# Gates and ups of the first feed-forward by seven block products from the third pair of tiles on

## The chip, the cores and the metric

One Trainium2 chip; the kernel runs on one of its cores. The metric is the time of one execution on the device, in microseconds (us), as the median of several runs.

## The reference

One layer of an encoder on 784 tokens (16 meta tokens, 512 of a prompt, 256 of a sample), model width 1024, feed-forward width 2816, all in float32. What matters here, shortened:

```python
def rmsnorm(x, w):
    return x * lax.rsqrt(jnp.mean(x * x, axis=-1, keepdims=True) + EPS) * w

def swiglu(u, wg, wu, wd):
    return (jax.nn.silu(u @ wg) * (u @ wu)) @ wd

h += 0.5 * swiglu(rmsnorm(h, w1), wg1, wu1, wd1)     # first feed-forward, 784 tokens
u = rmsnorm(h, w_mix)                                # mixer: attention and a state space model
h += concat(diff_attention(u ...), ssd_mixer(u ...)) @ w_out
h += 0.5 * swiglu(rmsnorm(h, w2), wg2, wu2, wd2)     # second feed-forward, 768 tokens
y = rmsnorm(h, w_final)
```

## The kernel before

Features lie on the partitions, tokens along the free axis. The model width is 8 tiles of 128 (k), the feed-forward width 22 tiles in 11 pairs. The tokens are cut into two halves of 392 columns in the first feed-forward (784 tokens) and of 384 in the second (768).

**Products.** A float32 product is three matmuls of rounded numbers: each operand is split into a high part (ACT casts, line 182) and a low part (DVE subtracts, line 183), and `mm3` (lines 316 to 318) issues high x high, low x high and high x low. One unit of a gate or up is one feature tile by one token half: 8 k tiles, 24 matmuls into one PSUM bank (`ps_mm` or `ps_x`).

**Weights.** `Weights` loads them by SP's DMA queue in pieces of 512 KB (`wr`, two buffers) and splits them into `wh` and `wl` (four buffers). `pump`, called by `done()` after every unit, splits one job ahead when buffers are free. `done()` also moves every generator on the `agenda` one step: the norms, parameters and transfers that run beside the products. The order on an engine follows from this order of the program, which a scheduler lays out by priority.

**First feed-forward**, `ffn`. The activation goes into the products as h times the norm's weight (tiles `u1`); the token's factor (`rms1`, tile `w3_136` in the order) is multiplied in behind the gate: DVE multiplies (line 453), ACT does silu (454), DVE multiplies again (455). Ups: DVE multiplies the gate by the up (460) and the result is split into high and low parts. `BOUNDS` puts the pairs into groups [0], [1, 2], [3, 4], [5, 6], [7, 8], [9, 10]. The down product of a group comes after the first pair of the next group, and DVE adds it to h (line 480). Pair 0 runs on three parts of the tokens (272, 256, 256 columns), since the tokens are only just being loaded and normed.

**Second feed-forward**, `ffn_fast`. The first pair is plain; the others go through `quad`, which takes a block of two feature tiles, two halves of k and two token halves and computes it from seven products of 12 matmuls instead of eight (`p1`, `p6`, `p5`, `p2`, `p7`, `p3`, and `p4`, which is issued behind the first product of the next block). It needs sums of weight blocks (jobs `a` to `d` of `split_fast`, sums on DVE in lines 255 to 260) and of activation blocks (`t2`, `n1`, `m3`, `m4`, built once in `FastNorm.chain`), and combines the products on DVE (lines 652 to 688). A group's down product follows directly on its blocks (line 699).

**Memory.** One pool per stretch of the program: tags `w3`, `w4`, `f3` and so on in the pool `mix`, which lasts from the start to the second feed-forward's end.

**Parameters.** `parameters()` loads the small inputs, makes the lambda products (lines 925, 926), the relative position table `fv` (lines 930 to 932, 31 small copies) and its eight spread copies `fr_d` (520 KB each), all on the agenda of the first feed-forward.

Of the kernel before, what the change touches and what calls it, by code (L numbers as in the profile page):

```python
# [14 lines left out]
P = 128  # L15
# [32 lines left out]
def body(tc, x_prompt, x_sample, meta_tokens, ffn1_norm_w, ffn1_w_gate, ffn1_w_up, ffn1_w_down,  # L48
# [34 lines left out]
    next_stretch("mix")  # L83
# [4 lines left out]
    def f3(n, dt=F32):  # L88
        return stretch_pool[0].tile([P, XW + 1], dt, tag="f3", name="f3", bufs=18)[:, :n]

# [30 lines left out]
    BOUNDS = [0, 1, 3, 5, 7, 9, NPAIR]  # L121
# [19 lines left out]
    def plan_ffn_fast(f, wg, wu, wd):  # L141
        for g in range(len(BOUNDS) - 1):
            for pr in range(BOUNDS[g], BOUNDS[g + 1]):
                for key, src in (("g", wg), ("u", wu)):
                    (plan_fast if pr else plan_w8)((f, key, pr), src, pr * 256)
            plan_down(f, wd, g)

    def plan_ffn(f, wg, wu, wd):
        for g in range(len(BOUNDS) - 1):
            for i, pr in enumerate(range(BOUNDS[g], BOUNDS[g + 1])):  # L150
                plan_w8((f, "g", pr), wg, pr * 256)
                plan_w8((f, "u", pr), wu, pr * 256)
                if i == 0 and g > 0:
                    plan_down(f, wd, g - 1)
        plan_down(f, wd, len(BOUNDS) - 2)

    def plan_down(f, wd, g):
        k0, k1 = 2 * BOUNDS[g], 2 * BOUNDS[g + 1]
        for cp in range(KD // 2):
            plan_1((f, "d", g, cp), wd, k0, k1 - k0, cp * 256, 256)  # L160
# [18 lines left out]
    plan_ffn_fast(2, ffn2_w_gate[0], ffn2_w_up[0], ffn2_w_down[0])  # L179
# [17 lines left out]
    class Weights:  # L197
# [43 lines left out]
        def split_fast(self, key, kind, raw, hi, lo):  # L241
# [99 lines left out]
    def diags(r, tiles):  # L341

        dg = w3()
# [86 lines left out]
    def ffn(f, h, halves, u, after, first=None, last=None, rms=None):  # L430

        g_t = {}

        def gate_up(pr):
            sg = {}
            w = {}
            parts = (first or halves) if pr == 0 else halves
            end = len(parts) - 1

            def unit(which, m, i):  # L440
                o, n = parts[i]
                if which not in w:
                    w[which] = W.get8((f, "gu"[which], pr))
                ps = ps_any()
                dense(ps[:, :n], w[which], m, u(i if pr == 0 else None), o, n)
                if which == 0:
                    if i == 0:
                        sg[m] = w3()
                    t = sg[m][:, o:o + n]
                    if rms is None:  # L450
                        S.activation(t, ps[:, :n], AF.Silu)
                    else:
                        V.tensor_tensor(t, ps[:, :n], rms[:, o:o + n], ALU.mult)  # L453
                        S.activation(t, t, AF.Silu)  # L454
                        V.tensor_tensor(t, t, rms[:, o:o + n], ALU.mult)
                else:
                    if i == 0:
                        g_t[2 * pr + m] = [w4(T1, F32R), w4(T1, F32R)]
# [1217 lines left out]
```

## Time and profile before

| | |
|---|---|
| median of 3 runs | 1880.02 us (1877.45 to 1881.81) |
| the profiled execution | 1877.39 us |
| its span in the trace | 1875.7 us |
| mean granted clock of TensorE | 0.991 of full speed |
| busy share of the span: PE, DVE, ACT, POOL | 97%, 63%, 40%, 5% |
| first feed-forward | from about 20 to 575 us |
| second feed-forward | from about 1330 us to the end |

The profile is of one execution. PE is TensorE's matmuls, DVE VectorE, ACT ScalarE, POOL GpSimd, SP the engine that issues the DMAs here. A group of instructions has a line of the kernel, an operation, its tiles (out<-in), a count, busy time and mean duration, and the idle time of the engine ahead of its members with the engine that ended most of it. A duration is that of one instruction; neighbours overlap, so the distance of their starts is shorter.

### The profile page before, as it was taken

The numbers are of one execution on the slowest core, as the hardware profiler recorded it, in microseconds if no ns is written. First come the engines' busy times: TensorE is split into PE (matmuls) and PEld (weight loads), VectorE is DVE, ScalarE is ACT, GpSimd is POOL, SyncE is SP. The second block draws the span as 40 slices with busy tenths as digits, with TensorE's granted clock in tenths as the row PEclk, the third lists the DMA queues.
The fourth block names the chain that finished last, engine by engine and source line by source line (L and its number), as shares of the span: only waits on it lengthen the run. The fifth ranks groups of instructions, "written<-read, shape, count | busy, mean of one in ns | idle before, by whom it ended". The sixth has DMA issues, their size and how long they took to land.

```text
span 1875.7 us, 27520 instructions
## 1 busy us (share of the span) xinstructions
PE 1825.0 (97%) x10934; PEld 1756.2 (94%) x10934; DVE 1175.6 (63%) x2305; ACT 748.2 (40%) x1486; POOL 93.8 (5%) x118
## 2 busy tenths in 40 slices
PE   7999999999999999989899999999999999999998
PEld 7999999999998998878798988999989999999997
DVE  6454333443436489676787878674897575757573
ACT  6222121212123452667556767343334241414144
POOL 0000000000003000123100000001100000000002
PEclk9999999999999999999899999999999999999999
DMA  4152212221222223797541334321112121222121
GB/s 139 58 172 68 66 47 68 68 61 52 71 64 93 68 65 93 184 232 202 161 140 50 89 98 151 134 88 43 35 57 90 46 90 53 83 57 80 56 79 68
DMA packets 161268, 169.77 MB, mean 91 GB/s; under 512 B 9921, under 2 KB 146234, under 8 KB 161138
## 3 DMA queue, kind: packets, MB, share of 16 engines
q1 hardware_dynamic: 161122, 168.00, 29.9%
q8 instruction: 86, 1.41, 0.3%
q14 instruction: 44, 0.36, 0.1%
q10 hardware_dynamic: 16, 0.00, 0.0%
HBM read 148.54 MB, written 22.87 MB: 91 GB/s over the span
## 4 chain that ended last, share of the span: by engine, by line
PE 83%; DVE 10%; ACT 3%; issue 2%; DMA 2%; POOL 0%; SPq 0%; ACTq 0%; POOLq 0%; DVEq 0%
PE ps_mm L316 13%; PE ps_mm L317 13%; PE ps_mm L318 13%; PE ps_x L316 10%; PE ps_x L318 10%; PE ps_x L317 9%; PE ps_s L316 2%; PE ps_s L317 2%; PE ps_s L318 2%; DVE w L1026 2%; PE ps_s L1462 2%; DMA w<-ar_d 1%; PE ps_s L1580 1%; ACT w L1209 1%; DVE wl L183 1%
## 5 line engine op out<-in xcount | busy, mean ns | idle before, releaser
L316 PE MATMUL ps_mm<-w,wh 128*128 128x384 f32 (+4 forms) x1520 | 518.7, 341 | 4.0 <-DVE w L1341 1.9
L317 PE MATMUL ps_mm<-w,wl 128*128 128x384 f32 (+4 forms) x1520 | 515.5, 339 | 4.3 <-DVE wl L183 4.3
L318 PE MATMUL ps_mm<-w,wh 128*128 128x384 f32 (+4 forms) x1520 | 516.5, 340 | 2.8 <-DVE w L183 2.2
L182 ACT CAST wh<-wr 128x1024 fp32r<-128x1024 f32 (+1 forms) x194 | 190.1, 981 | 312.0 <-PE ps_x L318 251.2
L316 PEld LDWEIGHTS ps_mm<-w,wh 128*128 128x128 f32 x1520 | 287.2, 189 | 10.7 <-issue 2.7
L316 PE MATMUL ps_x<-w,wh 128*128 128x392 f32 (+4 forms) x864 | 293.7, 340 | 0.9 <-ACT w L1107 0.9
L318 PEld LDWEIGHTS ps_mm<-w,wh 128*128 128x128 f32 x1520 | 287.1, 189 | 7.4 <-DVE w L183 3.3
L317 PEld LDWEIGHTS ps_mm<-w,wl 128*128 128x128 f32 x1520 | 287.3, 189 | 7.0 <-DVE wl L183 4.6
L317 PE MATMUL ps_x<-w,wl 128*128 128x392 f32 (+4 forms) x864 | 292.8, 339 | 0.0
L318 PE MATMUL ps_x<-w,wh 128*128 128x392 f32 (+4 forms) x864 | 292.3, 338 | 0.0
L183 DVE TENSOR_TENSOR wl<-wr,wh 128x1024 fp32r<-128x1024 f32 (+1 forms) x194 | 222.1, 1146 | 87.6 <-ACT wh L182 86.8
L316 PEld LDWEIGHTS ps_x<-w,wh 128*128 128x128 f32 x864 | 163.7, 189 | 2.1 <-ACT w L1107 1.2
L317 PEld LDWEIGHTS ps_x<-w,wl 128*128 128x128 f32 x864 | 163.8, 190 | 0.7
L318 PEld LDWEIGHTS ps_x<-w,wh 128*128 128x128 f32 x864 | 163.5, 189 | 0.7
L182 ACT CAST w<-w 128x392 fp32r<-128x392 f32 (+4 forms) x130 | 73.8, 570 | 202.4 <-DVE w L460 118.3
L183 DVE TENSOR_TENSOR w<-w,w 128x392 fp32r<-128x392 f32 (+4 forms) x130 | 83.4, 645 | 29.4 <-ACT w L182 28.5
L365 POOL TENSOR_TENSOR w<-w,w 128x392 f32<-128x392 f32 (+3 forms) x36 | 40.7, 1130 | 981.7 <-ACT w L364 981.7
L182 ACT CAST wh<-sums 128x1024 fp32r<-128x1024 f32 x40 | 42.0, 1051 | 108.7 <-PE ps_x L318 60.5
L1486 ACT ACTIVATE w<-w,nmx 128x528 f32<-128x528 f32 (+1 forms) x96 | 63.6, 664 | 40.0 <-DVE nmx L1482 31.0
L454 ACT ACTIVATE w<-w 128x392 f32<-128x392 f32 (+2 forms) x46 | 23.8, 516 | 112.8 <-DVE w L453 112.8
L183 DVE TENSOR_TENSOR wl<-sums,wh 128x1024 fp32r<-128x1024 f32 x40 | 49.0, 1225 | 29.6 <-ACT wh L182 29.6
L1209 ACT ACTIVATE w<-w,w 128x128 f32<-128x128 f32 x192 | 58.2, 389 | 15.4 <-POOL w L1205 15.4
(335 smaller groups left out, 2872.6 us busy)
## 6 DMA issues: line engine op xcount, KB each, us to landing
wr<-in_ffn_w_gate_dram SPq DMA_DIRECT2D x44, 512.0 KB
wr<-in_ffn_w_up_dram SPq DMA_DIRECT2D x42, 512.0 KB
wr<-in_w_in_dram SPq DMA_DIRECT2D x42, 512.0 KB
wr<-in_ffn_w_down_dram SPq DMA_DIRECT2D x40, 512.0 KB
w<-ar_d SPq DMA_DIRECT2D x24, 512.0 KB
wr<-in_w_out_dram SPq DMA_DIRECT2D x16, 512.0 KB
w<-ar_d SPq DMA_DIRECT2D x24, 256.0 KB
w<-q_d SPq DMA_DIRECT2D x32, 192.0 KB
```

The source lines that it names most:

```text
L182: a = S.copy(hi, src)
L183: return a, V.tensor_tensor(lo, src, hi.bitcast(F32), ALU.subtract)
L316: nc.tensor.matmul(ps, ah, bh, start=start, stop=False, skip_group_check=onto)
L317: nc.tensor.matmul(ps, al, bh, start=False, stop=False, skip_group_check=onto)
L318: last_mm[0] = nc.tensor.matmul(ps, ah, bl, start=False, stop=stop, skip_group_check=onto)
L365: G.tensor_tensor(sums[0], sums[0], sq, ALU.add)
L454: S.activation(t, t, AF.Silu)
L1026: V.scalar_tensor_tensor(acc, pad[:, j:j + XW], prmT[:, cw:cw + 1], acc, ALU.mult, ALU.add)
L1209: S.activation(ab[d][:, h, :], ab[d][:, h, :], AF.Exp, bias=ssm["asp"][:, c, col_s:col_s + 1])
L1462: nc.tensor.matmul(ps[:, b, :w], qh[c][part][:, P * i:P * i + P], kh[c][:, k0 + b * w:k0 + b * w + w], start=part == 0, stop=part == 1)
L1486: S.activation(e[:, :nk], e[:, :nk], AF.Exp, bias=nmx[:, c:c + 1], scale=-1.0, accum_out=(s0, s1)[c])
L1580: nc.tensor.transpose(ps[:n, 0, q * P:(q + 1) * P], A[q0 + q][:, c:c + n], ident)
```

## The change

One function `ffn` now serves both feed-forwards, as plain pairs first and then quads. `GROUPS` gives each its groups: the first feed-forward runs pairs 0 and 1 plain and pairs 2 to 10 as quads, the second as before. In the first, the gates keep their multiplication by the token's factor, now in `act`. A class `Blocks` builds the sums of the activations for the first feed-forward on the agenda, from the last part of pair 0 on, and writes `n1` over a part of `u1` behind pair 1. In `split_fast`, job `d` takes two sums instead of three by going on from job `b`'s. The memory of this stretch has a pool of its own (`f1s`, `f1g`, `f1t`), between one for the loading of the tokens and the mixer's. The lambda products use other tiles and come earlier; the table `fv` and the copies `fr_d` go from the first feed-forward to the mixer, behind `dt_unit`. The down product of a group follows directly on its blocks in both feed-forwards.

```diff
-    BOUNDS = [0, 1, 3, 5, 7, 9, NPAIR]
+    GROUPS = {1: [0, 2, 3, 5, 7, 9, NPAIR], 2: [0, 1, 3, 5, 7, 9, NPAIR]}
...
-                sums = stretch_pool[0].tile([P, 2 * 4 * P], F32, tag="sums", name="sums", bufs=1)
-                t = sums.rearrange("p (s k f) -> p s k f", s=2, k=4)
                 if kind == "b":
+                    sums = stretch_pool[0].tile([P, 2 * 4 * P], F32, tag="sums", name="sums", bufs=1)
+                    t = self.sums = sums.rearrange("p (s k f) -> p s k f", s=2, k=4)
                     V.tensor_tensor(t[:, 1], raw[0][:, :, y], raw[1][:, :, y], ALU.add)
                     V.tensor_tensor(t[:, 0], t[:, 1], raw[0][:, :, x], ALU.add)
                 else:
-                    V.tensor_tensor(t[:, 0], raw[0][:, :, x], raw[0][:, :, y], ALU.add)
-                    V.tensor_tensor(t[:, 1], raw[1][:, :, x], raw[1][:, :, y], ALU.add)
-                    V.tensor_tensor(t[:, 1], t[:, 0], t[:, 1], ALU.add)
+                    t, self.sums = self.sums, None
+                    V.tensor_tensor(t[:, 1], raw[0][:, :, x], raw[0][:, :, y], ALU.add)
+                    V.tensor_tensor(t[:, 0], t[:, 0], raw[1][:, :, x], ALU.add)
...
+        def act(t, src, o, n):
+            if rms is None:
+                S.activation(t, src, AF.Silu)
+            else:
+                V.tensor_tensor(t, src, rms[:, o:o + n], ALU.mult)
+                S.activation(t, t, AF.Silu)
+                V.tensor_tensor(t, t, rms[:, o:o + n], ALU.mult)
...
+        for pr in range(bounds[0], bounds[1]):
+            plain(pr)
+        norm.ready()
         down(0)
-        norm.B[1][:4] = [None] * 4
-        for g in range(1, len(BOUNDS) - 1):
+        for g in range(1, len(bounds) - 1):
             late = None
-            for pr in range(BOUNDS[g], BOUNDS[g + 1]):
+            for pr in range(bounds[g], bounds[g + 1]):
                 for which in range(2):
                     steps = quad(which, pr)
...
+    class Blocks:
...
+        def split(self, key, t, pair=None):
...
+            S.copy(hi, t)
+            V.tensor_tensor(lo, t, hi.bitcast(F32), ALU.subtract)
...
+        def first_sum(self, k):
+            a = f1(2 * self.n)
+            b12, n1 = a[:, :self.n], a[:, self.n:]
+            x, w = self.part(k, 1)
+            S.activation(b12, x, AF.Copy, scale=w)
+            x, w = self.part(k, 0)
+            V.scalar_tensor_tensor(n1, x, w, b12, ALU.mult, ALU.subtract)
+            return b12, n1
+
+        def sums(self):
+            for k in range(4):
+                m4, n1 = self.first_sum(k)
+                b = f1(2 * self.n)
+                t2, m3 = b[:, :self.n], b[:, self.n:]
+                x, w = self.part(k + 4, 1)
+                V.scalar_tensor_tensor(t2, x, w, n1, ALU.mult, ALU.add)
+                x, w = self.part(k, 0)
+                V.scalar_tensor_tensor(m3, x, w, t2, ALU.mult, ALU.subtract)
+                yield 1
+                x, w = self.part(k + 4, 0)
+                V.scalar_tensor_tensor(m4, x, w, t2, ALU.mult, ALU.subtract)
+                self.split("t2", t2)
+                yield 1
+                self.split("m3", m3)
+                self.split("m4", m4)
+                yield 1
+
+        def ready(self):
+            complete(self.made)
+            for k in range(4):
+                self.split("n1", self.first_sum(k)[1], self.B[1][k])
...
+            elif blocks.made not in agenda and not blocks.T:
+                xt.clear()
+                next_stretch("ffn1")
+                later(blocks.made)
...
-    ffn(1, h1, HALF1, u_first, nm.after, first=PARTS, rms=rms1)
+    ffn(1, h1, HALF1, blocks, nm.after, None, g_first, f1, u_first, PARTS, rms1)
+    next_stretch("mix")
...
     dt_unit(W.get8("dt"))
     for k in range(KD):
         nc.sync.dma_start(out=h_d[k], in_=h1[k][:, NMETA:T1])
+    later(distances())
```

How DVE's order changes at three places follows. `w3_136` is the token's factor, `wl` a low part of weights, `sums` a sum of weight blocks; what stands in brackets is what the row waits for.

DVE, the gate of a pair in the middle of the first feed-forward, before:

```order
L453 TENSOR_TENSOR w3_1256<-ps_mm_1231,w3_136 128x392 [waits PE_49]
L455 TENSOR_TENSOR w3_1256<-w3_1256,w3_136 128x392 [waits Activation_49]
L453 TENSOR_TENSOR w3_1256<-ps_x_1261,w3_136 128x392 [waits PE_49]
L455 TENSOR_TENSOR w3_1256<-w3_1256,w3_136 128x392 [waits Activation_49]
L453 TENSOR_TENSOR w3_1315<-ps_mm_1290,w3_136 128x392 [waits PE_49]
L455 TENSOR_TENSOR w3_1315<-w3_1315,w3_136 128x392 [waits Activation_49]
L183 TENSOR_TENSOR wl_1349<-wr_1150,wh_1348 128x1024 [waits DMAHW7_49,Activation_49]
L453 TENSOR_TENSOR w3_1315<-ps_x_1320,w3_136 128x392 [waits PE_49]
L183 TENSOR_TENSOR wl_1386<-wr_1196,wh_1385 128x1024 [waits DMAHW2_49,Activation_49]
L455 TENSOR_TENSOR w3_1315<-w3_1315,w3_136 128x392 [waits Activation_49]
```

And after, from the gate's second product to the weights of what follows (lines 526 and 528 are the two multiplications, 617, 635 and 641 the combinations of products):

```order
L617 TENSOR_TENSOR w3_2589<-ps_mm_2621,w3_2589 128x392 [waits DVE_49,PE_49]
L186 TENSOR_TENSOR wl_2636<-sums_2637,wh_2635 128x1024 [waits Activation_49]
L526 TENSOR_TENSOR w3_2588<-ps_s_2590,w3_136 128x392 [waits PE_49]
L263 TENSOR_TENSOR sums_2637<-wr_2584 128x512 [waits DVE_49]
L264 TENSOR_TENSOR sums_2637<-sums_2637,wr_2586 128x512
L528 TENSOR_TENSOR w3_2588<-w3_2588,w3_136 128x392 [waits Activation_49]
L635 TENSOR_TENSOR w3_2589<-ps_x_2657,w3_2589 128x392 [waits PE_49]
L526 TENSOR_TENSOR w3_2589<-w3_2589,w3_136 128x392 [waits DVE_49]
L528 TENSOR_TENSOR w3_2589<-w3_2589,w3_136 128x392 [waits Activation_49]
L641 TENSOR_TENSOR w3_2588<-ps_mm_2621,w3_2589 128x392 [waits PE_49]
L526 TENSOR_TENSOR w3_2588<-w3_2588,w3_136 128x392 [waits DVE_49]
L186 TENSOR_TENSOR wl_2691<-wr_2586,wh_2690 128x1024 [waits Activation_49]
```

A gate's two weight splits among eight multiplications have become splits and sums of weights between combinations and multiplications; in one place 526 and 528 of the same tile are neighbours.

DVE, pair 0's last part (256 columns), before:

```order
L460 TENSOR_TENSOR w3_339<-ps_x_599,w3_339 128x256 [waits PE_49]
L453 TENSOR_TENSOR w3_284<-ps_mm_627,w3_136 128x256 [waits PE_49,Activation_49]
L183 TENSOR_TENSOR w4_415<-w3_339,w4_414 128x256 [waits Activation_49]
L455 TENSOR_TENSOR w3_284<-w3_284,w3_136 128x256 [waits Activation_49]
L183 TENSOR_TENSOR wl_684<-wr_243,wh_683 128x1024 [waits DMAHW5_49,Activation_49]
```

And after (`f1t` holds the sums of u, `f1s` their split parts):

```order
L526 TENSOR_TENSOR w3_285<-ps_mm_628,w3_136 128x256 [waits Activation_49]
L938 SCALAR_TENSOR_TENSOR f1t_660<-w3_87,n1w_119,f1t_660 128x392 [waits Activation_49]
L528 TENSOR_TENSOR w3_285<-w3_285,w3_136 128x256 [waits Activation_49]
L947 SCALAR_TENSOR_TENSOR f1t_663<-w3_91,n1w_119,f1t_660 128x392 [waits DVE_49]
L949 SCALAR_TENSOR_TENSOR f1t_663<-w3_87,n1w_119,f1t_663 128x392 [waits DVE_49]
L549 TENSOR_TENSOR w3_340<-ps_x_600,w3_340 128x256 [waits PE_49]
L952 SCALAR_TENSOR_TENSOR f1t_660<-w3_91,n1w_119,f1t_663 128x392
L929 TENSOR_TENSOR f1s_701<-f1t_663,f1s_701 128x392 [waits Activation_49]
```

The sums of u stand between the activations and ahead of the next weight split.

DVE, the mixer's start, before:

```order
L183 TENSOR_TENSOR wl_5227<-wr_5163,wh_5226 128x1024 [waits DMAHW5_49,Activation_49]
L183 TENSOR_TENSOR wl_5269<-wr_5197,wh_5268 128x1024 [waits DMAHW6_49,DVE_49,Activation_49]
L183 TENSOR_TENSOR wl_5314<-wr_5230,wh_5313 128x1024 [waits DMAHW7_49,Activation_49]
L183 TENSOR_TENSOR wl_5381<-wr_5272,wh_5380 128x1024 [waits DMAHW0_49,PE_49,Activation_49]
L1063 COPY w3_5319<-ps_x_5322 128x192 [waits PE_49]
```

And after (the rows left out are more copies of line 897):

```order
L186 TENSOR_TENSOR wl_5404<-wr_5340,wh_5403 128x1024 [waits DMAHW4_49,Activation_49]
L186 TENSOR_TENSOR wl_5446<-wr_5374,wh_5445 128x1024 [waits DMAHW5_49,DVE_49,Activation_49]
L895 MEMSET w4_5496 8x1
L897 COPY w4_5496<-rbT_259 8x437
...
L897 COPY w4_5496<-rbT_259 8x421
L186 TENSOR_TENSOR wl_5491<-wr_5407,wh_5490 128x1024 [waits DMAHW6_49,Activation_49]
L186 TENSOR_TENSOR wl_5591<-wr_5449,wh_5590 128x1024 [waits DMAHW7_49,PE_49,Activation_49]
L1102 COPY w3_5529<-ps_x_5532 128x192 [waits PE_49]
```

The table's 31 copies have moved in ahead of the last two of these splits.

## Rows read from the trace of the kernel before

**Rows 1.** The page's shares, and the granted clock in 40 slices.

```profile
PE 1825.0 (97%) x10934; PEld 1756.2 (94%) x10934; DVE 1175.6 (63%) x2305; ACT 748.2 (40%) x1486; POOL 93.8 (5%) x118
PEclk9999999999999999999899999999999999999999
```

**Rows 2.** Stretches: busy us and instructions by engine, clock, DMA share, GB/s.

```profile
100.00:150.00 50.00, 50.00 (x282) 49.81 (x282) 23.33 (x36) 11.89 (x16) 0.00 (x0) 1.00 0.52 169
200.00:250.00 50.00, 50.00 (x282) 50.00 (x281) 19.38 (x28) 10.32 (x14) 0.00 (x0) 1.00 0.19 56
1400.00:1420.00 20.00, 20.00 (x115) 19.79 (x115) 14.68 (x21) 8.04 (x12) 0.00 (x0) 1.00 0.23 71
1420.00:1440.00 20.00, 20.00 (x116) 20.00 (x115) 17.21 (x28) 7.72 (x12) 0.00 (x0) 1.00 0.27 79
```

**Rows 3.** Groups of PE instructions, 100 to 560 us.

```profile
L316 PE MATMUL ps_mm<-w,wh 128*128 128x392 f32 x431 | 146.9, 341 | 0.0
```

**Rows 4.** Groups of PE instructions, 1395 to 1830 us.

```profile
L317 PE MATMUL ps_mm<-w,wl 128*128 128x384 f32 x210 | 70.9, 337 | 0.0
```

**Rows 5.** Timeline of DVE: start, duration, instruction, idle time before it.

```profile
113.29 0.57 DVE L453 TENSOR_TENSOR w<-ps_mm,w 128x392 f32<-128x392 f32 x1 [1.78 <-PE ps_mm L318]
...
571.58 0.57 DVE L480 SCALAR_TENSOR_TENSOR w<-ps_x,w 128x392 f32<-128x392 f32 x1 [1.58 <-PE ps_x L318]
...
1403.08 0.55 DVE L652 TENSOR_TENSOR w<-w,ps_s 128x384 f32<-128x384 f32 x1
...
1802.03 0.55 DVE L652 TENSOR_TENSOR w<-w,ps_s 128x384 f32<-128x384 f32 x1
```

**Rows 6.** Timeline of DVE in an unbroken row, second feed-forward.

```profile
1393.01 0.55 DVE L699 SCALAR_TENSOR_TENSOR w<-ps_mm,w 128x384 f32<-128x384 f32 x1
1393.48 0.55 DVE L699 SCALAR_TENSOR_TENSOR w<-ps_x,w 128x384 f32<-128x384 f32 x1
1393.94 0.68 DVE L258 TENSOR_TENSOR sums<-wr 128x512 f32<-128x512 f32 x1
1394.54 1.22 DVE L183 TENSOR_TENSOR wl<-wr,wh 128x1024 fp32r<-128x1024 f32 x1
1395.68 0.55 DVE L699 SCALAR_TENSOR_TENSOR w<-ps_mm,w 128x384 f32<-128x384 f32 x1
```

**Rows 7.** Groups of DVE instructions, 1395 to 1830 us.

```profile
L183 DVE TENSOR_TENSOR wl<-wr,wh 128x1024 fp32r<-128x1024 f32 x40 | 48.9, 1222 | 10.8 <-ACT wh L182 10.6
L183 DVE TENSOR_TENSOR wl<-sums,wh 128x1024 fp32r<-128x1024 f32 x39 | 47.8, 1225 | 29.4 <-ACT wh L182 29.4
L183 DVE TENSOR_TENSOR w<-w,w 128x384 fp32r<-128x384 f32 x40 | 22.1, 554 | 6.8 <-ACT w L182 6.4
L699 DVE SCALAR_TENSOR_TENSOR w<-ps_x,w 128x384 f32<-128x384 f32 x34 | 18.9, 555 | 31.2 <-PE ps_x L318 31.1
...
L255 DVE TENSOR_TENSOR sums<-wr 128x512 f32<-128x512 f32 x19 | 13.2, 692 | 11.8 <-DMA wr<-in_ffn_w_gate_dram 10.2 <-DMA wr<-in_ffn_w_up_dram 1.2
```

**Rows 8.** Groups of DVE instructions, 100 to 560 us.

```profile
L455 DVE TENSOR_TENSOR w<-w,w 128x392 f32<-128x392 f32 x36 | 20.4, 566 | 16.1 <-ACT w L454 16.1
```

**Rows 9.** Stretches of pair 0 and pair 1, columns as in rows 2.

```profile
40.00:60.00 20.00, 19.79 (x160) 19.61 (x160) 10.95 (x33) 6.92 (x13) 0.00 (x0) 1.00 0.19 54
60.00:80.00 20.00, 20.00 (x114) 20.00 (x113) 8.85 (x16) 5.07 (x9) 0.00 (x0) 1.00 0.19 57
```

**Rows 10.** PE's waits: us in total, times, the longest.

```profile
PE ps_mm L317 <- DVE wl L183: 4.3, 1, 4.3
```

**Rows 11.** Stretches around that wait, columns as in rows 2.

```profile
1360.00:1380.00 20.00, 15.71 (x86) 15.34 (x85) 20.00 (x43) 10.01 (x23) 0.00 (x0) 0.91 0.02 7
1380.00:1400.00 20.00, 20.00 (x108) 20.00 (x107) 16.14 (x28) 5.49 (x8) 0.00 (x0) 0.92 0.36 108
```

**Rows 12.** Timeline of DVE: copies of the table, first and last of 7 rows.

```profile
88.99 0.37 DVE L932 COPY w<-rbT 8x437 f32<-8x437 f32 x1
...
95.32 0.59 DVE L932 COPY w<-rbT 8x14 f32<-8x14 f32 x4
```

**Rows 13.** Timeline of DVE at the mixer's start.

```profile
639.51 1.22 DVE L183 TENSOR_TENSOR wl<-wr,wh 128x1024 fp32r<-128x1024 f32 x1 [2.64 <-ACT wh L182]
```

More of the change, by code (lines that the diff above doesn't have):

```diff
@@ L82, in body @@
     stretch_pool = [None]
-    next_stretch("mix")
+    next_stretch("tokens")
     def w4(n=1056, dt=F32):
@@ L573, in chain, with ffn @@
                 yield 1
-    def ffn_fast(f, h, halves, norm, after, last):
+    def ffn(f, h, halves, norm, after, last, new_g, new_up, first, parts=None, rms=None, ended=None):
+        bounds = GROUPS[f]
         g_t = {}
@@ new lines, in plain, with unit @@
+        def plain(pr):
+            ws = {}
+            pieces = (parts if pr == 0 else None) or halves
+            end = len(pieces) - 1
+            def unit(which, m, i):
+                o, n = pieces[i]
+                if which not in ws:
+                    ws[which] = W.get8((f, "gu"[which], pr))
+                ps = ps_any()
+                xs, c = first(i if pr == 0 else None, i)
+                dense(ps[:, :n], ws[which], m, xs, c, n)
+                if not i and not which:
+                    sg[2 * pr + m] = w3(h[0].shape[-1])
+                t = sg[2 * pr + m][:, o:o + n]
+                if which == 0:
+                    act(t, ps[:, :n], o, n)
+                else:
+                    V.tensor_tensor(t, ps[:, :n], t, ALU.mult)
+                    split_g(2 * pr + m, o, n)
+                done(2 if i == end and m else 0)
+            if pr == 0:
+                for i in range(len(pieces)):
+                    for which in range(2):
+                        for m in range(2):
+                            unit(which, m, i)
+            else:
@@ L590, in first @@
                 for which in range(2):
-                    if not i:
-                        ws[which] = W.get8((f, "gu"[which], 0))
                     for m in range(2):
-                        ps = ps_any()
-                        norm.get(i)
-                        dense(ps[:, :n], ws[which], m, norm.B[i], 0, n)
-                        if not i and not which:
-                            sg[m] = w3(T2)
-                        t = sg[m][:, o:o + n]
-                        if which == 0:
-                            S.activation(t, ps[:, :n], AF.Silu)
-                        else:
-                            V.tensor_tensor(t, ps[:, :n], t, ALU.mult)
-                            split_g(m, o, n)
-                        done(2 if i and m else 0)
+                        for i in range(len(pieces)):
+                            unit(which, m, i)
@@ L607, in quad @@
+            for m in range(2):
+                del sg[2 * pr + m]
         def quad(which, pr):
@@ L711, in down @@
                 ws = {}
-                for i, part in enumerate(last):
+                pieces = last or halves
+                for i, part in enumerate(pieces):
                     for m in range(KD):
@@ L717, in down @@
                         after(m, i)
-                        done(1 if m % 2 and i == len(last) - 1 else 0)
-        first()
-        norm.get(None)
+                        done(1 if m % 2 and i == len(pieces) - 1 else 0)
+            g_t.clear()
+        for pr in range(bounds[0], bounds[1]):
+            plain(pr)
+        norm.ready()
         down(0)
-        norm.B[1][:4] = [None] * 4
-        for g in range(1, len(BOUNDS) - 1):
+        for g in range(1, len(bounds) - 1):
             late = None
-            for pr in range(BOUNDS[g], BOUNDS[g + 1]):
+            for pr in range(bounds[g], bounds[g + 1]):
                 for which in range(2):
@@ L735, in ffn_fast @@
             late()
-            if g == len(BOUNDS) - 2:
-                next_stretch("end")
+            if g == len(bounds) - 2:
+                norm.over()
+                if ended:
+                    ended()
             down(g)
```

169 lines of the change are left out of this document (62 added, 107 removed).

## The prediction

> **What bounds the kernel now.** I started with the page's shares and slices. The reader is to see in them that TensorE (PE) is busy nearly the whole span while its granted clock stands at full speed almost everywhere; VectorE (DVE) comes far behind it [rows 1]. A share over the whole span says little about one stage, so I then read the busy times in stretches of the first feed-forward. PE is busy 50.00 of 50 us in each, at a granted clock of 1.00, with 282 matmuls, and DVE only 19 to 23 us [rows 2]. The groups of PE instructions between 100 and 560 us say the same from the other side: the idle time ahead of the six that carry this stage (one of them is shown, the others have the same 0.0) is 0.0 [rows 3]. So in this stage every matmul taken away is time taken away, until something else becomes the bound. Of that something the same kernel holds a sample: its second feed-forward already runs seven-product blocks, and there PE is again idle for 0.0 us ahead of its large groups, of which one is shown [rows 4], with DVE at 14.7 to 17.2 of 20 us in the stretches shown [rows 2].
>
> **What a matmul is worth.** The duration in the groups (341 ns) overlaps with the next matmul and is not the price. I take two moments instead. DVE's first activation of pair 2 starts at 113.29, as soon as that pair's first unit leaves PE; its last accumulation of the last down product's first half starts at 571.58 [rows 5]. Between them PE does the other 7 units of pair 2 (168 matmuls), 8 pairs of 192 (1536), four down products of 192 (768) and half of the last (96): 2568. So (571.58 - 113.29) / 2568 = 0.1785 us each, at 392 columns. The same in the second feed-forward: from pair 1's second product at 1403.08 to pair 10's at 1802.03 [rows 5] there are 9 pairs of 168 and 4 downs of 192, 2280 matmuls in 398.95 us, 0.1750 each at 384 columns. Per column this is 0.4553 ns in plain blocks and 0.4557 ns in seven-product blocks. The sample thus shows no loss per matmul from the seven-product form itself.
>
> **The removed work.** A pair's gate and up are 8 x 24 = 192 matmuls in plain form and 2 x 7 x 12 = 168 in the other. Pairs 2 to 10 change, so 9 x 24 = 216 go. TensorE's order of before and after, counted row by row, differs by just that. 216 x 0.1785 = **38.5 us** off.
>
> A page of the Trainium skill, "TensorE: Matmul & The Clock Gate", section Back-to-back issue gap, gives N / 2.4 + 2.5 ns for an isolated warm matmul, which at 392 columns is 165.8 ns; the sum would then be 35.8 us off. The trace has 178.5 ns for the same thing, and that is what I use.
>
> **The added work on DVE, per pair.** The prices are starts in an unbroken row, not durations: an operation of 384 columns lasts 0.55 us, but the next starts 0.47 us later; one of 512 columns lasts 0.68 and holds the engine 0.60; one of 1024 lasts 1.22 and holds it 1.14 [rows 6]. For 392 columns, whose duration is 0.566 us against 0.555 [rows 8, 7], I scale 0.47 to 0.48. A block needs for its weights one split of 512 columns, three of 1024 and now four sums: 0.60 + 3.42 + 2.40 = 6.42 us. Its activations are 13 operations of 392 columns, in a gate 5 combinations and 8 rms multiplications, in an up 6, 3 products and 4 splits: 6.24 us. Together 12.66 per block and 25.3 per pair, against 168 x 0.1785 = 30.0 us of PE: 84%. The same count for the second feed-forward gives 22.5 of 29.4 (77%), and there it costs PE nothing. So the new load is heavier than the sample, by 2.8 us a pair, but under the limit. The down products between the groups give DVE more air. I take 0 here; its upper bound is the first rival.
>
> The waits within a gate block are what the sample doesn't have. DVE multiplies, ScalarE (ACT) does silu, DVE multiplies again. In the order after, one of the four halves has its two multiplications right behind each other, so DVE stands still there until silu is done; in before such a wait is 16.1 / 36 = 0.45 us [rows 8]. Behind it are queued the next product's subtraction and a weight split. 0.45 us lies well inside the 2.3 us per block that DVE has left, so it stays hidden unless it falls on a split that is due.
>
> **The new sums of u.** They are built between pair 0's last part and the end of pair 1: 4 x 7 DVE operations of 392 columns, 13.4 us, with 4 x 2 more (3.9 us) before the quads. Before, DVE has 10.95 and 8.85 of 20 us busy there [rows 9], so there is room, but a split of pair 1's weights can now stand behind up to three of these sums (about 1.4 us, and more with ACT's copies ahead of them). The nearest row is the same kind of build in the second feed-forward, where PE waited 4.3 us once for a weight's low part [rows 10]. Bounds 0 and 4; I take 1, nearer to 0 because DVE there was full (20.00 of 20 [rows 11]) and here is half empty.
>
> **What is moved.** The relative position table (31 small copies, 3.1 us of DVE in 7 pieces [rows 12], and eight 520 KB transfers on SP's queue) goes from the first feed-forward to the mixer. Where it came from nothing waits on PE's path, so nothing is won. Where it goes, the copies stand in DVE's order ahead of two weight splits; one of that row's splits waited 2.64 us for ACT there [rows 13], so most of 3.1 is covered. Bounds 0 and 3; I take 0.5. The lambda products move forward, to the time when their transfers have only just been issued; DVE can wait there for the landing: bounds 0 and 2, taken as 0, since PE has work queued. A group's down product now follows directly on the group's last block, whose last half needs subtraction, product, ACT's cast and the low part (some 2.2 us by the durations of these rows) before PE can use it. The other half comes first, 24 matmuls or 4.3 us, which covers it. With six such places I put 0.5 us, bounds 0 and 4.
>
> **The sum.** The profiled execution took 1877.39 us: 1877.39 - 38.5 + 1 + 0.5 + 0 + 0.5 = 1840.9. That execution lies 2.6 us under the median of the runs (1880.02), so for a median I state **1843**. Without any of the small losses it is 1841; with all of them at their upper bounds (4 + 3 + 2 + 4 = 13) 1854.
>
> **Rivals.** (a) The gate blocks stall on DVE. For it: 84% load, and four multiply-silu-multiply chains per block that the sample doesn't have. With all four waits open a block has 12.66 + 4 x 0.45 = 14.5 of 15.0 us, so any uneven moment reaches PE. I price that at 1 to 2 us per gate block, two to four of those waits: 9 x (1 to 2) = 9 to 18 us on top, 1852 to 1861. Against it: four buffers of split weights and PSUM banks that let PE run ahead.
>
> (b) The sums of u delay pair 1's weights so that PE stops long enough for its clock to fall. In the second feed-forward that stop cost 4.3 us [rows 10], and the granted clock was 0.91 and 0.92 in the two stretches around it [rows 11]; (0.09 + 0.08) x 20 = 3.4 us more. Together 7.7 in place of the 1 in my sum: 1850.
>
> (c) Slower than before: DVE becomes the bound of all quads, because its waits do not overlap with its work but add to it. The waits per pair, from the rows: for ACT's weight casts and for the g split (10.6 + 29.4 + 6.4) / 10 = 4.6, for raw weights 11.8 / 10 = 1.2 [rows 7], for silu 8 x 0.45 = 3.6 [rows 8]. 25.3 + 9.4 = 34.7 us a pair against 30.0 of PE: 4.7 x 9 = 42 us, all of the gain and more, 1885. The point from which it decides: a pair of 30.0 + 38.5 / 9 = 34.3 us gives no gain. Against it: these idle times in the second feed-forward stand beside PE rows with 0.0 idle [rows 4]; they are DVE being ahead, not late.
>
> The Trainium skill's "VectorE: DVE Perf Modes", section Terms, speaks for (c): every DVE operation is followed by a pipeline flush, and the next can't issue before the pipe is empty. With full durations a pair would hold DVE 28.8 of 30.0 us (96%) in place of 25.3, and (c) would be the likeliest case, at about 9 x 8.2 = 74 us lost. The trace disagrees for independent neighbours: starts 0.47 us apart for durations of 0.55 [rows 6].
>
> (d) The change doesn't remove the matmuls: excluded by the count of TensorE's rows above.
>
> **How the numbers follow.** Forecast, with small losses from none to the middle of their bounds: 0.80. Rival (a) 0.10, (b) 0.05, (c) 0.03, and 0.02 for a mix of (a) and (c) that ends near 1877. Predicted is the forecast's 1843. The range goes from 1836 (no loss, 1841, less half of the 4.4 us by which the runs of before differ, and a little for a stage that runs smoother) to 1860 (all small bounds at their ends, or most of rival (a)); it leaves out (c), the mix and the top of (a). A measurement of this kernel can tell about 0.2% (3.8 us) from no change. Only (c) ends above 1884, the mix falls within: faster 0.95, same 0.02, slower 0.03.
>
> **What would show it.** In the profile after, PE should have 216 matmuls fewer, idle 0.0 ahead of its groups in the quads, a quad pair of 30.0 us between equal points, and the last down's first half should end 36 to 38 us earlier than at 571.58. DVE should be near 84% in the quads and still show idle time for ACT's casts. Rival (a) would show as PE idle behind DVE's subtractions or splits once in each gate block; (b) as one PE wait between 55 and 75 us and a clock under 1.00 behind it; (c) as pairs of 34 us or more with DVE near 100%. The forecast is wrong if pairs take over 31 us though PE has its 168 matmuls, or if the mixer, otherwise unchanged, grows by more than 3 us.

## The result, and the profile after

The changed kernel takes 1848.32 us (median of 4 runs, 1847.48 to 1853.35) against 1879.72 of before (4 runs, 1877.45 to 1881.81): a ratio of 0.9839, with a 95% interval from 0.9818 to 0.986, or 31 us less. A later series gave 1848.51 (5 runs). The prediction said 1843, in a range from 1836 to 1860. The direction and the main term are right; some 5 us are missing, and one cause, which stood in the prediction at a price of 0, accounts for most of them. One run of the version with late lambda products, described below, was slow (3540.36 us) and is left out of that version's numbers.

The page of the profile after begins its part 1 with this line; compare [rows 1]. PE has 10718 matmuls, 216 fewer than 10934:

```profile
PE 1795.0 (97%) x10718; PEld 1722.8 (93%) x10718; DVE 1302.6 (70%) x2519; ACT 797.2 (43%) x1564; POOL 96.2 (5%) x118
```

The profiled execution took 1853.35 us with a span of 1851.6, the longest of its four, so it shows a little more loss than the median has. The same points of the program, in the profiles of before and after:

| point | before, us | after, us | after minus before |
|---|---|---|---|
| pair 1, PE's first matmul | 57.23 | 63.91 | +6.7 |
| pair 1, DVE takes PE's first unit | 62.41 | 70.32 | +7.9 |
| last down, end of the first half | 571.58 | 541.70 | -29.9 |
| mixer, copy behind `dt_unit` | 645.7 | 615.7 | -30.0 |
| state space stage, last exponential | 903.0 | 876.6 | -26.4 |
| norm of the second feed-forward, start | 1320.4 | 1294.5 | -25.9 |
| end of the span | 1875.7 | 1851.6 | -24.1 |

Between PE's first matmul of pair 1 and the end of the last down's first half lies the work from which the 38.5 us were taken: it became 36.6 us shorter. But PE began it 6.7 us later. DVE took pair 1's first unit another 1.2 us later, because a weight split and sums of u stood ahead of it in DVE's order; PE went on without idle time there. The points themselves are rows of the timelines of PE and DVE (start, duration, instruction, idle time before it and what ended it). Of before, with [rows 5] for 571.58:

```profile
57.23 0.34 PE L316 MATMUL ps_mm<-w,wh 128*128 128x392 f32 x1
...
62.41 0.56 DVE L453 TENSOR_TENSOR w<-ps_mm,w 128x392 f32<-128x392 f32 x1
```

Of after, the first two rows are pair 1's, the next two are the same place in the gates of pairs 2 and 10, the last is the end of the last down's first half:

```profile
63.91 0.34 PE L320 MATMUL ps_mm<-w,wh 128*128 128x392 f32 x1
...
70.32 0.56 DVE L526 TENSOR_TENSOR w<-ps_mm,w 128x392 f32<-128x392 f32 x1
...
141.61 0.56 DVE L526 TENSOR_TENSOR w<-ps_s,w 128x392 f32<-128x392 f32 x1
...
503.33 0.56 DVE L526 TENSOR_TENSOR w<-ps_s,w 128x392 f32<-128x392 f32 x1
...
541.70 0.57 DVE L658 SCALAR_TENSOR_TENSOR w<-ps_x,w 128x392 f32<-128x392 f32 x1 [1.58 <-PE ps_x L322]
```

From pair 2's gate to pair 10's there are 8 pairs of 168 matmuls and down products of 672: 2016, which at the predicted 0.1785 us take 359.8 us. The rows say 361.7. So the quads with their group borders lose 1.9 us against an unbroken row of matmuls, no more, and that is the whole difference between 38.5 and 36.6. The groups of PE between 60 and 540 us say it too (busy us, mean ns, idle us ahead); they answer to [rows 3]:

```profile
L320 PE MATMUL ps_mm<-w,wh 128*128 128x392 f32 x264 | 90.0, 341 | 0.4 <-ACT w L185 0.4
L321 PE MATMUL ps_mm<-w,wl 128*128 128x392 f32 x264 | 89.8, 340 | 0.0
...
L320 PE MATMUL ps_s<-w,wh 128*128 128x392 f32 x144 | 49.2, 341 | 0.5 <-DVE w L611 0.4
```

On DVE, from 100 to 525 us, the waits that the slower rival counted are there, but they are waits of an engine that is ahead (answers to [rows 8] and, for the weights, [rows 7]):

```profile
L186 DVE TENSOR_TENSOR wl<-sums,wh 128x1024 fp32r<-128x1024 f32 x36 | 44.1, 1225 | 19.8 <-ACT wh L185 19.8
...
L528 DVE TENSOR_TENSOR w<-w,w 128x392 f32<-128x392 f32 x36 | 20.3, 563 | 6.1 <-ACT w L527 5.6
...
L258 DVE TENSOR_TENSOR sums<-wr 128x512 f32<-128x512 f32 x18 | 12.5, 692 | 9.5 <-DMA wr<-in_ffn_w_gate_dram 7.4 <-DMA wr<-in_ffn_w_up_dram 1.6
```

Now the 6.7 us ahead of pair 1. PE's waits between 15 and 80 us (total, times, longest) are in before, first, and after, second:

```profile
PE ps_x L353 <- DVE w L345: 1.1, 2, 0.9
```

```profile
PE ps_x L357 <- DVE w L349: 5.0, 2, 4.7
```

The matmul that waits (line 357) spreads the tokens' norm factor for the next part of the tokens; DVE makes its input in a chain of small operations (lines 765, 337 to 342, 349). DVE's timeline of after shows what that chain stood behind:

```profile
30.01 0.07 DVE L754 MEMSET xss<- 128x2 f32 x2
34.23 0.23 DVE L888 TENSOR_TENSOR B<-B 128x64 f32<-128x64 f32 x1 [4.15 <-DMA B<-in_lambda_k_dram]
35.20 0.22 DVE L888 TENSOR_TENSOR B<-B 128x64 f32<-128x64 f32 x1 [0.75 <-DMA B<-in_lambda_k_dram]
35.34 0.21 DVE L889 TENSOR_REDUCE lam<-B 128x1 f32<-128x64 f32 x1
35.47 0.43 DVE L549 TENSOR_TENSOR w<-ps_x,w 128x272 f32<-128x272 f32 x1
```

These are the lambda products, which the change moved ahead. DVE stands idle for 4.9 us until their small vectors have landed; SP issues the last of them here, at 32.35 us:

```profile
26.55 1.83 SPq L862 DMA_DIRECT2D B<-in_lambda_k_dram  x1
30.79 0.33 SPq L862 DMA_DIRECT2D B<-in_lambda_q_dram  x1
32.35 0.33 SPq L862 DMA_DIRECT2D B<-in_lambda_k_dram  x1
```

The stop of PE is only part of the price. The stretches (busy us by engine, clock, DMA share, GB/s), first one of before, then three of after (40 to 60 us answers to [rows 9]), show 3.94 us without a matmul and then a clock of 0.83, where before has 1.00:

```profile
20.00:40.00 20.00, 19.10 (x160) 18.90 (x160) 14.63 (x48) 14.44 (x37) 0.00 (x0) 1.00 0.20 56
```

```profile
20.00:40.00 20.00, 16.06 (x134) 15.85 (x133) 11.95 (x40) 8.41 (x21) 0.00 (x0) 1.00 0.23 62
40.00:60.00 20.00, 18.97 (x136) 18.80 (x137) 15.20 (x46) 13.00 (x30) 0.00 (x0) 0.83 0.00 1
60.00:80.00 20.00, 20.00 (x125) 20.00 (x124) 18.54 (x35) 10.56 (x20) 0.00 (x0) 1.00 0.34 106
```

PE's idle time in the first 40 of these us is 5.0 us, against 1.1 before (20 - 19.10 from 20 to 40 us, and 0.2 in [rows 9]); 0.17 x 20 = 3.4 us come from the clock. 3.9 + 3.4 = 7.3; PE came to pair 1 6.7 us later than before, and 7.8 us later than in an execution of this kernel without the wait (56.14 us, the last experiment).

### The profile page after: what moved, and what is told of

It reads as the page before. It is cut to its first block, busy times and chain, and to the rows that moved or that the text cites. A ratio compares the mean times of both kernels' runs of the same rounds, so it can differ in the third digit from the quotient of the medians.

```text
span 1851.6 us, 27377 instructions
## 1 busy us (share of the span) xinstructions
PE 1795.0 (97%) x10718; PEld 1722.8 (93%) x10718; DVE 1302.6 (70%) x2519; ACT 797.2 (43%) x1564; POOL 96.2 (5%) x118
## 4 chain that ended last, share of the span: by engine, by line
PE 78%; DVE 12%; ACT 4%; DMA 3%; issue 2%; POOL 0%; SPq 0%; DVEq 0%; POOLq 0%; ACTq 0%
PE ps_mm L321 12%; PE ps_mm L320 12%; PE ps_mm L322 12%; PE ps_x L320 8%; PE ps_x L322 8%; PE ps_x L321 8%; PE ps_s L320 4%; PE ps_s L321 4%; PE ps_s L322 4%; DVE w L1064 2%; PE ps_s L1501 2%; DVE wl L186 2%; PE ps_s L1619 1%; ACT w L1248 1%; DMA w<-ar_d 1%
## 5 line engine op out<-in xcount | busy, mean ns | idle before, releaser
L320 PE MATMUL ps_mm<-w,wh 128*128 128x384 f32 (+3 forms) x1296 | 441.4, 341 | 6.1 <-DVE w L1380 2.1
L321 PE MATMUL ps_mm<-w,wl 128*128 128x384 f32 (+3 forms) x1296 | 439.0, 339 | 5.4 <-DVE wl L186 5.4
L322 PE MATMUL ps_mm<-w,wh 128*128 128x384 f32 (+3 forms) x1256 | 426.1, 340 | 2.7 <-DVE w L186 2.2
L320 PEld LDWEIGHTS ps_mm<-w,wh 128*128 128x128 f32 x1296 | 244.9, 189 | 13.3 <-ACT w L185 3.0
L322 PEld LDWEIGHTS ps_mm<-w,wh 128*128 128x128 f32 x1256 | 237.2, 189 | 7.4 <-DVE w L186 3.0
L320 PE MATMUL ps_x<-w,wh 128*128 128x392 f32 (+4 forms) x496 | 169.4, 341 | 0.9 <-ACT w L1146 0.9
L321 PE MATMUL ps_x<-w,wl 128*128 128x392 f32 (+4 forms) x496 | 168.2, 339 | 0.0
L322 PE MATMUL ps_x<-w,wh 128*128 128x384 f32 (+4 forms) x456 | 154.7, 339 | 0.0
L320 PE MATMUL ps_s<-w,wh 128*128 128x384 f32 (+1 forms) x304 | 103.4, 340 | 1.4 <-DVE w L611 0.8
L322 PE MATMUL ps_s<-w,wh 128*128 128x384 f32 (+1 forms) x304 | 103.0, 339 | 0.0
L321 PE MATMUL ps_s<-w,wl 128*128 128x384 f32 (+1 forms) x304 | 103.0, 339 | 0.0
L320 PEld LDWEIGHTS ps_x<-w,wh 128*128 128x128 f32 x496 | 95.9, 193 | 2.0 <-ACT w L1146 1.2
L321 PEld LDWEIGHTS ps_x<-w,wl 128*128 128x128 f32 x496 | 95.9, 193 | 0.7
```

Source lines behind the costliest of these rows:

```text
L320: nc.tensor.matmul(ps, ah, bh, start=start, stop=False, skip_group_check=onto)
L321: nc.tensor.matmul(ps, al, bh, start=False, stop=False, skip_group_check=onto)
L322: last_mm[0] = nc.tensor.matmul(ps, ah, bl, start=False, stop=stop, skip_group_check=onto)
```

## The experiments

All kernels are the changed one with the edit shown, except where it says the kernel before.

**The changed kernel again.**

> The changed kernel once more, beside the others on the same chip. Both theories: 1846 to 1850 us; it gives the scatter against which the next runs are read. In the profile DVE again waits 4 to 5 us for the lambda vectors near 30 us and PE stops behind it.

1848.51 us (1846.23 to 1851.27, 5 runs). In its profile PE comes to pair 1 at 61.97, 4.7 us later than before, and DVE takes the first unit at 67.56, 5.2 later; the two lambda products waited 3.21 and 0.67 us for their DMA. So PE's loss at the start is 5 to 7 us, as the landing falls.

**Lambda products late.** The four operations are put behind one on the same engine that comes later (they start at 124.84 us instead of 34.23); their transfers stay:

```diff
-        V.tensor_scalar(subw, prmT[:, sub0:sub0 + 1], 1.0 - LAM_INIT, None, ALU.mult)
-        for i in range(2):
+        ins = V.tensor_scalar(subw, prmT[:, sub0:sub0 + 1], 1.0 - LAM_INIT, None, ALU.mult)
+        with behind([ins]):
+            for i in range(2):
...
```

> The four small lambda operations are queued on DVE behind the operation that makes subw, some 75 us later; their transfers stay where they are. Theory (the early lambda products cost the missing time): DVE's wait of 4.9 us near 30 us is gone, PE has no stop of 4.7 us there, the clock between 40 and 60 us is 1.00 and not 0.83, the first unit of pair 1 ends near 62.4 us instead of 70.3, and the time falls by 7 to 8 us to about 1840.5. Rival (the new sums of u, or the second memory pool, delay pair 1 whatever the lambda products do): at least half of the loss stays, 1844 to 1848, and a wait of PE for a weight's low part shows between 55 and 70 us.

1845.3 us in this series (median of 1841.92, 1844.49, 1846.16 and 1846.5), 3.2 under the changed kernel beside it. The profile is that of 1846.16, with a span of 1844.4. Its stretches, and its rows for pair 1 and for the end of the last down's first half, with the last one of before behind them:

```profile
20.00:40.00 20.00, 20.00 (x166) 19.86 (x166) 15.38 (x49) 12.38 (x33) 0.00 (x0) 0.99 0.23 63
40.00:60.00 20.00, 19.59 (x159) 19.41 (x158) 16.45 (x44) 11.41 (x23) 0.00 (x0) 1.00 0.18 53
```

```profile
57.33 0.34 PE L320 MATMUL ps_mm<-w,wh 128*128 128x392 f32 x1
...
63.50 0.56 DVE L526 TENSOR_TENSOR w<-ps_mm,w 128x392 f32<-128x392 f32 x1
...
535.22 0.57 DVE L372 TENSOR_TENSOR w<-w 128x392 f32<-128x392 f32 x1
```

```profile
572.18 0.57 DVE L368 TENSOR_TENSOR w<-w 128x392 f32<-128x392 f32 x1
```

PE's stop and the fall of the clock behind it are gone. PE comes to pair 1 at 57.33 instead of 63.91 (57.23 in before), and the row behind the last down's first half is at 535.22, where before has it at 572.18: 37.0 of the 38.5 us are there. Up to this point the theory holds but for DVE's row of pair 1 (63.50, not 62.4), and on PE nothing is left for the rival (the sums of u delaying pair 1) but 0.1 us. But only part of it reached the end in this execution: the end of the span is 31.3 us earlier, not 37, and the time misses the expected 1840.5. What is lost behind the first feed-forward is followed below.

**Lambda transfers first.** Products in their place of the change, transfers issued ahead of the other parameters:

```diff
         V.memset(prm, 0.0)
+        lqk = [small([P, P], "B", 4).rearrange("p (i d) -> p i d", i=2) for _ in range(2)]
+        for i, src in enumerate((lambda_q1, lambda_k1, lambda_q2, lambda_k2)):
+            rep(lqk[i // 2][:, i % 2, :], src[0], P)
...
```

> The lambda products stay where the change put them, but their transfers are issued ahead of all other parameters. Theory (DVE waits for the landing): the wait is gone or under 1 us, and the time is that of the run with late products, 1840 to 1842. Rival (the place of the products in DVE's order costs, not the landing): the time stays at 1847 to 1849. What could spoil it: the two weight transfers between the parameters come up to 4 us later, which would show as a wait of PE for pair 1's weights.

1851.01 us (1849.6 to 1856.36): neither got its way, and the profile says why. With the transfers earlier, the scheduler put the products earlier too, into the chain that norms the first tokens; the wait came back at the start of the kernel. DVE, and the PE row that waited on it:

```profile
17.97 0.23 DVE L888 TENSOR_TENSOR B<-B 128x64 f32<-128x64 f32 x1 [6.67 <-DMA B<-in_lambda_k_dram]
```

```profile
19.71 0.60 PE L321 MATMUL ps_mm<-w,wl 128*128 128x272 f32 x1 [7.64 <-DVE wl L186]
```

SP issued these transfers from 9.34 to 12.49 us, so a product waited until 5.5 us after the last issue. The wait is thus for the landing and follows the products to where the scheduler puts them; the expectation was wrong in taking the products' place as fixed.

**Two more sums a block.** On top of the late products:

```diff
+                    for _ in range(2 if key[0][0] == 1 else 0):
+                        V.tensor_tensor(t[:, 1], raw[0][:, :, y], raw[1][:, :, y], ALU.add)
                     V.tensor_tensor(t[:, 1], raw[0][:, :, y], raw[1][:, :, y], ALU.add)
```

> Late lambda products, and two more operations of 512 columns on DVE in each block of the first feed-forward (a sum of job b repeated twice, with the same result): 1.2 us a block by the distance of starts, 36 in all, 21.6 us of DVE. Theory (a block takes 12.66 us of DVE against 15.0 of PE, waits are slack): 13.9 of 15.0, no loss over 2 us against the run with late products alone. Rival (DVE's waits add to its work, so that its blocks are already at or near the limit): the added time shows in full, 1.2 to 1.4 us a block, 21 to 25 us more.

1843.7 us (1840.64 to 1846.25), not above the run without the sums. The first row is the end of the last down's first half, to be held against 535.22 (PE comes to pair 1 at 57.41 here and at 57.33 there); the second is PE's only wait between 75 and 540 us:

```profile
535.25 0.57 DVE L374 TENSOR_TENSOR w<-w 128x392 f32<-128x392 f32 x1
```

```profile
PE ps_mm L322 <- ACT w L185: 0.4, 1, 0.4
```

21.6 us of work on DVE cost 0.0 us. So a block has at least 1.2 us of DVE to spare, which fits the 2.3 us of the prediction and excludes the rival.

The Trainium skill's "VectorE: DVE Perf Modes", section Terms, says that the next operation can't issue until the pipe behind the last one is empty. Read by itself it would have DVE held for full durations: an estimate of 28.8 / 2 + 2 x 0.69 = 15.8 us per block here, against 15.0 of PE, and 14 us lost in 18 such blocks. This run, with 0.0, disagrees.

**Five more sums a block.** The same with 5 for 2.

> Late lambda products, and five more operations of 512 columns on DVE in each block of the first feed-forward: 3.0 us a block, 54 us in all. Theory (12.66 us a block by the distance of starts): 15.7 of 15.0 us, so a pair is short by 1.4 us, which the split weights in four buffers and the down product behind every second pair make up in part; 0 to 12 us over the run with late products, with the first PE waits for DVE's combinations or splits inside the quads. Rival (waits add to the work; the block is nearer to full): 25 us or more over it.

1849.94 us (1847.8 to 1850.88). Now PE waits inside the quads, between 75 and 540 us (first four of its waits), the last down's first half ends 7.7 us later than with the late products alone, though PE had come to pair 1 0.5 us earlier (56.81), and one stretch shows 3.7 us without a matmul, with DVE busy for 44.55 of the 50 us:

```profile
PE ps_s L322 <- ACT wh L185: 2.0, 2, 1.2
PE ps_s L323 <- DVE wl L186: 1.7, 2, 1.0
PE ps_mm L323 <- DVE wl L186: 1.1, 3, 0.4
PE ps_mm L322 <- ACT w L185: 0.4, 1, 0.4
```

```profile
542.92 0.57 DVE L374 TENSOR_TENSOR w<-w 128x392 f32<-128x392 f32 x1
```

```profile
200.00:250.00 50.00, 46.30 (x255) 44.73 (x254) 44.55 (x72) 17.89 (x25) 0.00 (x0) 1.00 0.27 85
```

54 us of added work cost 8, inside the 0 to 12 that the count by distances of starts gave. What a block has to spare lies between 1.2 and 3.0 us; the predicted 15.0 - 12.66 = 2.3 is inside, and these two runs say no more than that.

**The kernel before, again.**

> The kernel before once more, for a second profile of its state space stage (between 700 and 930 us). In the first profile of before that stage ran its twelve products with no fall of the clock from 755 to 900 us, in four of five profiles of the changed kernel and its variants it fell there once or twice, 3 to 5 us each run. Theory (these falls are scatter of a stage that waits for its transfers): this profile may show one as well, the runs scatter over 4 us or more as before. Rival (the change causes them): no fall between 755 and 900 us here either.

1880.88 us (1877.94 to 1889.41, 10 runs). Its profile has no fall of the clock between 755 and 900 us either, as before's first (a stretch of 145 us at 1.00); it has one at 715 to 725 us, as the first. The five profiles of the changed kernel and its variants that were there at the time all show falls between 755 and 900 us by their stretches, not four of five. So this run fits the rival; all profiles are counted together below.

**The table alone.** The kernel before, with `fv` and `fr_d` moved to the mixer:

```diff
...
         nc.sync.dma_start(out=h_d[k], in_=h1[k][:, NMETA:T1])
+    later(distances())
...
```

> The kernel before with one part of the change alone: the table fv and its eight copies fr_d go from the first feed-forward to the mixer; no quads, no new layout. Theory (the move costs nothing, as the mixer's start shows the same times before and after it): 1878 to 1883, within 0.2% of before. Rival (the copies' 4 MB in the mixer push the state space stage, which lives on transfers, into waits and a lower clock): 4 to 6 us more, 1884 to 1888, with falls of the clock between 755 and 900 us.

1882.93 us (1878.57 to 1887.35, 11 runs), a ratio of 1.0007 [0.9998, 1.0016] to before. The mixer's copy behind `dt_unit` starts at 645.7 us as in before, and in the state space stage one fall of the clock shows:

```profile
L1065 DVE COPY w<-ps_x x1: 358/358/358, 645.7 to 645.7; 128x192 f32<-128x192 f32 x1
```

```profile
800.00:805.00 5.00, 4.62 (x39) 4.48 (x40) 5.00 (x9) 4.32 (x13) 1.19 (x1) 0.66 0.33 88
```

This fall takes 1.7 us, as much as the one that before has at 715 to 725 us and that is missing here. The move costs between 0 and 3 us; 4 to 6 are excluded.

**Lambda products late, again.**

> The version with the late lambda products once more, for its scatter: 1841 to 1846.5 us. Theory (what is left of the difference to 1841 is the clock in the state space stage): the runs lie in two heaps some 4 us apart, and a profile without falls of the clock between 720 and 860 us has a span under 1841. Rival (a steady loss elsewhere): a profile without these falls still has a span of 1843 or more.

1842.23 us (1841.75 to 1846.61). The eight runs of this version that are compared, from two chips on which before took 1881.63 and 1881.22, lie between 1841.75 and 1842.24 (four), at 1844.49, and between 1846.16 and 1846.61 (three); their median is 1843.4. The span of this profile is 1840.0. The last exponential of the state space stage is 37.4 us earlier than in before, in the other profile of this version 34.4. Where the difference arises is seen in the stretches, first of the other profile (span 1844.4), then of this one:

```profile
760.00:765.00 5.00, 3.29 (x33) 3.15 (x33) 4.30 (x4) 4.65 (x14) 0.49 (x1) 0.66 0.30 88
765.00:800.00 35.00, 32.11 (x246) 30.13 (x245) 26.19 (x35) 21.17 (x60) 8.80 (x8) 1.00 1.03 256
800.00:805.00 5.00, 5.00 (x38) 2.89 (x39) 1.75 (x6) 4.50 (x14) 0.98 (x1) 0.71 0.60 195
805.00:810.00 5.00, 5.00 (x22) 4.71 (x20) 3.52 (x4) 1.40 (x2) 0.00 (x0) 0.60 0.00 0
```

```profile
760.00:765.00 5.00, 2.74 (x26) 2.77 (x28) 4.84 (x5) 5.00 (x16) 1.03 (x1) 0.72 0.44 113
765.00:800.00 35.00, 33.74 (x264) 31.20 (x260) 24.68 (x35) 20.27 (x57) 10.03 (x8) 0.99 1.01 259
800.00:865.00 65.00, 63.46 (x445) 54.32 (x441) 44.93 (x57) 52.06 (x116) 21.48 (x16) 1.00 0.73 197
```

The stage takes its rows by DMA at a share of 1.0, PE waits there by turns, and in the first profile the clock stood at 0.71 and 0.60 for 10 us behind such a turn: (0.29 + 0.40) x 5 = 3.5 us, and the other profile has none of it. Between the mixer's copy (607.13 and 607.65) and the last exponential (868.6 and 865.6) the first profile falls back by just these 3.5 us; another 1.3 of the 4.4 us between the spans arise from there to the norm of the second feed-forward, with equal falls of the clock. So the theory of two heaps holds in the main, with one run between the heaps, and the profile without this fall has a span under 1841.

## Why the prediction was right, and where it was off

**Right: the price of a matmul and their number.** 216 matmuls at 0.1785 us, 38.5 us. From PE's first matmul of pair 1 to the end of the last down's first half, 36.6 of it was there in the changed kernel, and without the lambda wait 37.1 and 36.9; the 1.9 us of the quads and their borders are what is missing.

**Right: DVE's load by distances of starts, and that waits hide.** Quads lose 1.9 us with their borders; 0.5 and 0 were taken. Two and five added sums put the limit into a range that holds the count's. Rival (a), PE stalls once per gate block, is not there: 0.5 us of idle ahead of the `ps_s` products shown, 0.4 of it for DVE. Rival (c) is not there either.

**Right: the moved table.** 0.5 was taken, 0.0 measured at the place that was named (-29.9 ahead of it, -30.0 behind it); 0 to 3 by the runs of the table alone.

**Too high by what shows: the sums of u.** With the lambda wait gone PE comes to pair 1 at 56.14 or 57.33 us, against 57.23 in before: -1.1 to +0.1, for a term of 1. That distance alone does not price them, since the changed kernel begins pair 0 earlier (11.19 against 15.52 us); but PE waits for no sum and no weight there. Its only wait from 15 to 75 us, in the execution with 56.14, is for the norm factor:

```profile
PE ps_x L357 <- DVE w L349: 0.4, 1, 0.4
```

The 1.2 us between these two executions lie ahead of the sums. Matmuls of 272 columns start 0.23 us apart at first and 0.125 later, and the second distance begins at 20.5 us in the profile with 57.33 and at 18.2 in the one with 56.14. PE's matmuls from 18 to 20 us are 11 in the first and 18 in the second:

```profile
18.00:20.00 2.00, 2.00 (x11) 2.00 (x10) 1.81 (x3) 1.00 (x2) 0.00 (x0) 0.50 0.08 1
```

```profile
18.00:20.00 2.00, 2.00 (x18) 2.00 (x17) 1.51 (x2) 0.75 (x1) 0.00 (x0) 1.00 0.09 1
```

**Wrong in its size: the lambda products.** The step was "DVE can wait there for the landing: bounds 0 and 2, taken as 0, since PE has work queued". Measured: 4.9 us of wait on DVE, 4.7 on PE and a lowered clock behind it; PE came to pair 1 6.7 us late in this profile and 4.7 in another, and in medians the kernel with the wait takes 5 us more (1848.5 of nine runs, 1843.4 of eight without it). Two things failed in it. The bound came from nothing in the trace that has the size of this landing. And PE's queue was thought full, while the next thing in it was a product that needs the tail of DVE's queue: the norm factor of the next tokens. The question behind "who waits for that" was answered with work that is queued, instead of with the next instruction in PE's order and its input. Rival (b) had this mechanism, a stop and then a lower clock, and its price (7.7), but at another place, pair 1's weights, which were on time: PE waits for no weight between 15 and 80 us.

**Not foreseen: what came behind the first feed-forward.** Of the profile's lead, 3.6 us went between the mixer's copy and the state space stage's last exponential, and 1.8 us in the second feed-forward. One of the prediction's own signs of being wrong is met by this, a mixer that grows by more than 3 us: from the last down's first half to the norm of the second feed-forward it grew by 4.0 us in this profile, and by 0.8 in that of the late products again. Against the 3.6 us stand 1.7 of a lower clock and 2.3 of idle PE (12.65 us there instead of 10.32). The stage is one which the change does not touch, in which the clock falls in some executions and not in others: (1 - clock) x time, from the mixer's convolutions to the fall at the stage's end that all profiles share, is 1.7 us in both profiles of before and in the one with the table moved, 1.7 in two of the changed kernel and its variants, 3.4 in two, 5.2 in one and 6.8 in two. Whether the changed kernel meets it more often by its nature, or by where its stretches happen to fall, these runs do not settle; the table's copies are not the cause by themselves. The last 1 to 2 us went in the second feed-forward (-25.9 at its norm, -24.1 at the end; -37.2 and -35.7 with the late products again). In the changed kernel's profile 0.9 of them are two waits of PE for a combination on DVE, which before does not have:

```profile
PE ps_s L320 <- DVE f L611: 0.5, 1, 0.5
PE ps_s L320 <- DVE w L611: 0.4, 1, 0.4
```

The cause of these waits is open: job `d` is one sum shorter there and two products have changed weights, which no run here undid.

So 1843 was the time of a kernel without the lambda wait: that version runs at 1842 to 1846.6, with a median of 1843.4. The kernel that was measured is this one with 5 us on top. That the sum fits so closely without the wait is in part luck: the quads cost 1.9 us where 0.5 stood, the sums of u and the table next to nothing where 1.5 stood, and 1 to 2 us in the second feed-forward stood nowhere.

## What to carry to other kernels

Where matmuls stand in an unbroken row, take their price from two moments and the count between them; the gain of removing some was met here to 5 per cent (36.6 to 37.1 of 38.5 us), as long as the next engine has been counted by the distance of its starts. The danger of a change like this lies less in the large work that it adds than in a small one that it moves: an operation of 0.2 us that waits for a transfer is worth as much as everything queued behind it, and it pays twice if the stop lowers TensorE's clock. For each operation that changes its place, look up the next row of its engine that another engine needs, and put it behind something that is late anyway when its input comes by DMA.

## What the runs showed of the hardware

Four vectors of 64 numbers, each spread to 128 partitions (128 KB in all), were issued from 25.69 to 32.68 us behind a 512 KB weight transfer, and the second product that reads them started at 35.20: 9.5 us from the first issue to the last use, of which SP's issuing took 7.0. Issued at the kernel's start, from 9.34 to 12.49 us, they let the first product start at 17.97, 8.6 us after the first issue.

A stop of PE of 4.7 us was followed by a granted clock of 0.83 over the next 20 us (0.50 from 40 to 45 us), one of 3.7 us (the changed kernel again) by 0.91.

The clock column can't be relied on in the first 20 us. In the changed kernel's profile it says 1.00 there, yet matmuls of 272 columns start 0.23 us apart until 19.3 us and 0.125 from 19.5 us on. Where PE had stopped for 7.6 us at the start (the lambda transfers first) it says 1.00 too, and the short distance begins only at 25.2 us.
